# w_ffn_in in 1024-column blocks, with three of eight pairs of K blocks in seven products, and half of their weight sums by accumulating DMA

## The chip, the cores and the metric

The kernel runs on one core of a Trainium2 chip. Its engines are TensorE (matmul; PE in the profile), VectorE (DVE), ScalarE (ACT), GpSimd (POOL) and SyncE (SP); DMAs are issued from the queues of SP, ACT and POOL. The metric is the time of one execution in device microseconds.

## The reference

One layer over 256 tokens of width 2048, all in float32: three gated token mixers with an output projection and a layer norm, then a SwiGLU feed forward of width 5632 and a layer norm. The change lies in the feed forward:

```python
x = layer_norm(DEEPNORM_ALPHA * x + mix, ln_mix_g[l], ln_mix_b[l])
h_gate, h_up = jnp.split(jnp.einsum('bsd,df->bsf', x, w_ffn_in[l]), 2, axis=-1)
ffn = jnp.einsum('bsf,fd->bsd', jax.nn.silu(h_gate) * h_up, w_ffn_out[l])
x = layer_norm(DEEPNORM_ALPHA * x + ffn, ln_ffn_g[l], ln_ffn_b[l])
```

## The kernel before

Every weight passes once through a stream. `load_one` (L98) loads a tile `wraw` of two K blocks of 128 rows by 512 columns, 512 KB, on SP's queue into one of four buffers. `split_one` (L87) splits it exactly into two float32r tiles: ScalarE casts the high part `whi` (L92), VectorE subtracts it from the weight for the low part `wlo` (L94); each has seven buffers. A product of activations and weights is then three matmuls (L118 to L120): high by high, high by low, low by high, with the stationary operand from the transposed activations (`th`, `tl`), and 512 weight columns streamed.

`gemm` (L139) takes one chunk of 512 columns over all of K, for both tiles of 128 tokens: at each weight tile it calls `pump`, which puts loads (five tiles ahead) and splits (three ahead) into the program, and then emits 12 matmuls, 2 K blocks x 2 token tiles x 3. At the chunk's end it evacuates the two PSUM banks. `defer` puts other work behind a number of weight tiles. A Tile scheduler orders the instructions of each engine; an engine then takes its own in that order, and waits at each for what it needs.

The feed forward has three parts (FF_PARTS) of four, four and three rounds. In a round, a gate chunk (`fg`, 16 K blocks) gives silu(gate) (L631, L632), an up chunk (`fu`) multiplies it (L640), and four transposes for each token tile put the result, split, into `hT` (L162 to L169). After the rounds of a part, four chunks of `w_ffn_out` (`fo`) add to the residual R (L652). In the first four rounds `mix_residual` (L617, L618) scales R. Six PSUM banks serve the chunks, two the transposes.

Of the kernel before, what the change touches and what calls it, by code (L numbers as in the profile page):

```python
# [8 lines left out]
F32 = mybir.dt.float32  # L9
F32R = mybir.dt.float32r  # L10
# [28 lines left out]
FF_PARTS = ((0, 4), (4, 8), (8, 11))  # L39

# [7 lines left out]
def trunk_kernel(ctx: ExitStack, tc: tile.TileContext, x, ln_in_g, ln_in_b, w_in, gate_bias,  # L48
# [10 lines left out]
    ps_acc = ctx.enter_context(tc.tile_pool(name="ps_acc", bufs=6, space=PSUM))  # L59
    ps_tp = ctx.enter_context(tc.tile_pool(name="ps_tp", bufs=2, space=PSUM))  # L60
# [22 lines left out]

    raw_t, split_t = {}, {}
    state = {"dma": 0, "split": 0}
    background = []

    def split_one():
        j = state["split"]
        t = raw_t.pop(j)  # L90
        hi = wp.tile([P, KT, NW], F32R, name="whi")
        nc.scalar.copy(out=hi, in_=t)  # L92
        lo = wp.tile([P, KT, NW], F32R, name="wlo")
        (nc.gpsimd if j in POOL_SPLIT else nc.vector).tensor_tensor(out=lo, in0=t, in1=hi.bitcast(F32), op=ALU.subtract)  # L94
        split_t[j] = (hi, lo)
        state["split"] += 1
# [7 lines left out]

    def pump(i):
# [5 lines left out]
        while state["split"] < min(len(plan), i + 1 + SPLIT_AHEAD):  # L111
            split_one()
        for _ in range(min(BACKGROUND, len(background))):
            background.pop(0)()
# [20 lines left out]
    def gemm(key, xs, evac, skew=0):  # L135
        """One 512-column chunk for both token tiles; the second one trails by `skew` weight tiles."""
        first_tile, nk = chunk[key]
        xh, xl = xs
        ps = [ps_acc.tile([P, NW], F32, name="acc") for _ in range(NT)]  # L139
        n = nk // KT  # L140
        for i in range(n + skew):
            if i < n:
                pump(first_tile + i)
            for t, ii in ((0, i), (1, i - skew)):
                if not 0 <= ii < n:
                    continue
                hi, lo = split_t[first_tile + ii]
                for kk in range(KT):
                    k = ii * KT + kk
                    mm_tile(ps[t], xh, xl, t, k, hi, lo, kk, k == 0, k == nk - 1)  # L150
                if ii == n - 1:
                    evac(t, ps[t])
            clock[0] += 1
            run_deferred()
        for i in range(n):
            split_t.pop(first_tile + i)

    def transpose4(src):
        """src [128, 4, 128] -> its four blocks transposed, in one bank."""
        tp = ps_tp.tile([P, 4, P], F32, name="tp")  # L160
# [52 lines left out]
    for f0, f1 in FF_PARTS:  # L213
        for f in range(f0, f1):
            add_chunk(("fg", f), w_ffn_in[0], f * NW, 0, 16)
            add_chunk(("fu", f), w_ffn_in[0], DFF + f * NW, 0, 16)
        for j in range(4):
            add_chunk(("fo", f0, j), w_ffn_out[0], j * NW, f0 * 4, (f1 - f0) * 4)

# [31 lines left out]
    cw = const.tile([P, 8, KC + KA], F32, name="cw")  # L251
    wT = const.tile([P, 8, P], F32, name="wT")
# [4 lines left out]
    # The tensor engine's clock rises only while it works.  # L257
# [11 lines left out]
    def norm_transposed(dst, q, t, src, mu, rs, pg, pb, out_xhat, act=2):  # L269
        """(src - mu) * rs, transposed, then * g + b per channel, split into dst."""  # L270
# [3 lines left out]
        y = blocks(new_tmp())  # L274
# [291 lines left out]
    ffp = None  # L566
    R, x2T = [], []

    def open_ffn():
        nonlocal ffp  # L570
        br.close()
        ffp = ctx.enter_context(tc.tile_pool(name="ffp", bufs=1))
        x2T.extend(new_xt(ffp))
        R.extend(ffp.tile([P, D], F32, name=f"R{t}") for t in range(NT))

    defer(open_ffn)

# [7 lines left out]
    for j in range(4):  # L585
        res = {}

        def residual(j=j, res=res):
            gj, bj = bcast(lg2, j, "gj"), bcast(lb2, j, "bj")
# [9 lines left out]
        def evac_o(t, ps, j=j, res=res):  # L599
# [4 lines left out]
            if j == 3:  # L604
                mu, rs = mean_rstd(stm[t])
                for q in range(4):
                    r_ = R[t][:, cols(q)]
                    norm_transposed(x2T, q, t, r_, mu, rs, PR_MG, PR_MB, r_)
# [3 lines left out]

    def mix_residual(j):
        gj, bj = bcast(ln_mix_g, j, "gj"), bcast(ln_mix_b, j, "bj")
# [6 lines left out]
    stf = stats_tile("stf", 4)  # L621
    f_ln = []
    for f0, f1 in FF_PARTS:
        hT = new_xt(act)
        last_part = f1 * NW == DFF
        for f in range(f0, f1):
            a_ = {}

            def evac_fg(t, ps, a_=a_):
                s_ = a_[t] = new_tmp()  # L630
                nc.scalar.activation(out=s_, in_=ps, func=AF.Sigmoid)  # L631
                nc.vector.tensor_tensor(out=s_, in0=ps, in1=s_, op=ALU.mult)  # L632

            gemm(("fg", f), x2T, evac_fg, skew=SKEW if f == 0 else 0)
            if f < 4:
                defer(lambda f=f: mix_residual(f))

            def evac_fu(t, ps, a_=a_, f=f):
                a = a_[t]
                nc.vector.tensor_tensor(out=a, in0=ps, in1=a, op=ALU.mult)  # L640
                defer(lambda: split_to(hT, 4 * (f - f0), t, transpose4(blocks(a))))

            gemm(("fu", f), x2T, evac_fu)
        if last_part:
            for src in (ln_ffn_g, ln_ffn_b):
                t_ = ffp.tile([P, D], F32, name="fln", bufs=2)
                nc.scalar.dma_start(out=t_, in_=src[0:1].broadcast_to([P, D]))
                f_ln.append(t_)
        for j in range(4):
            def evac_fo(t, ps, j=j):  # L650
                r_ = R[t][:, cols(j)]
                nc.vector.tensor_tensor(out=r_, in0=r_, in1=ps, op=ALU.add)  # L652
                if not last_part:
                    return
                nc.vector.bn_stats(out=stf[t][:, j, :], in_=r_)
                if j < 3:
                    return
                mu, rs = mean_rstd(stf[t])
                for q in range(4):
                    r_ = R[t][:, cols(q)]  # L660
                    nc.vector.scalar_tensor_tensor(out=r_, in0=r_, scalar=mu, in1=f_ln[0][:, cols(q)],
                                                   op0=ALU.subtract, op1=ALU.mult)
                    nc.vector.scalar_tensor_tensor(out=r_, in0=r_, scalar=rs, in1=f_ln[1][:, cols(q)],  # L663
                                                   op0=ALU.mult, op1=ALU.add)
                    (nc.sync, nc.scalar)[q % 2].dma_start(out=out2d[cols(t, P), cols(q)], in_=r_)

            gemm(("fo", f0, j), hT, evac_fo, skew=SKEW_OUT if last_part and j == 3 else 0)
# [30 lines left out]
```

## Time and profile before

| | |
|---|---|
| Time, median of three runs (range) | 1583.06 us (1582.04 to 1583.98) |
| Profiled execution: span from first to last instruction | 1580.9 us |
| TensorE busy | 1558.3 us, 99% |
| VectorE, ScalarE, GpSimd busy | 988.3 us (63%), 669.7 us (42%), 16.7 us |
| DMA | 308.1 MB, 195 GB/s |

The profiled execution is known by its span; the timed runs hold some two microseconds more. Matmuls are pipelined, so the mean time of one in the profile overlaps with the next; its pace is read from the distance of two events. A row of idle time names what an engine waited for last. The engine that is busy nearly all the time sets the end; waits of the others cost nothing as long as it does not wait for them.

### The profile page before, as it was taken

Reading aid. Unit: us, or ns where it says so; the run is one execution under the profiler, and the core shown is the slowest. Engines: PE = TensorE matmul, PEld = TensorE weight load, DVE = VectorE, ACT = ScalarE, POOL = GpSimd, SP = SyncE. Lnnn points to the kernel's source line nnn. Section 1 sums busy time; section 2 is a strip of 40 time slices with the busy share of each in tenths; the row PEclk is TensorE's granted clock in tenths of the full one; section 3 lists DMA queues with packets and bytes.
Section 4 is the critical chain, followed back from the end, with each engine's and each line's share of the span. In section 5 each row is a group of like instructions: output and inputs, shape, how many; then the busy total and the mean of one; then the engine's idle time right before and its main releaser. Section 6 shows DMA issues by size and latency. Waiting matters only on the chain.

```text
span 1580.9 us, 18324 instructions
## 1 busy us (share of the span) xinstructions
PE 1558.3 (99%) x6970; PEld 1280.5 (81%) x6970; DVE 988.3 (63%) x1216; ACT 669.7 (42%) x733; POOL 16.7 (1%) x28
## 2 busy tenths in 40 slices
PE   7999999999999999999999999999999999999997
PEld 4888888888888888888887888888888888888885
DVE  7699999455465555656769655555455554554465
ACT  5444444434444434544336444433444434344431
POOL 1000000000000000000000000000000000000000
PEclk9999999999999999999999999999999999999998
DMA  6866666666666666676866666666666666666652
GB/s 200 284 190 188 185 187 197 200 192 180 199 186 194 205 200 195 198 235 184 286 194 205 202 192 187 187 193 193 190 187 188 185 193 190 198 187 188 186 186 79
DMA packets 159278, 308.10 MB, mean 195 GB/s; under 512 B 9812, under 2 KB 10932, under 8 KB 158934
## 3 DMA queue, kind: packets, MB, share of 16 engines
q1 hardware_dynamic: 153942, 295.38, 62.2%
q10 hardware_dynamic: 5248, 11.55, 2.3%
q8 instruction: 54, 0.88, 0.2%
q14 instruction: 34, 0.28, 0.0%
HBM read 304.80 MB, written 2.10 MB: 194 GB/s over the span
## 4 chain that ended last, share of the span: by engine, by line
PE 97%; DVE 1%; DMA 0%; issue 0%; ACT 0%; POOL 0%; SPq 0%; POOLq 0%; DVEq 0%
PE acc L120 32%; PE acc L118 32%; PE acc L119 31%; PE tp L162 2%; DMA x<-in_x_dram 0%; PE tp L452 0%; DVE tmp L280 0%; DVE tmp L271 0%; DVE tl L169 0%; ACT tmp L278 0%; DVE wlo L94 0%; POOL ve L177 0%; DVE R L663 0%; DVE R L271 0%; PE tp L409 0%
## 5 line engine op out<-in xcount | busy, mean ns | idle before, releaser
L94 DVE TENSOR_TENSOR wlo<-wraw,whi 128x1024 fp32r<-128x1024 f32 x551 | 673.0, 1223 | 556.1 <-ACT whi L92 555.4
L92 ACT CAST whi<-wraw 128x1024 fp32r<-128x1024 f32 x552 | 580.7, 1053 | 835.8 <-PE acc L120 746.9
L118 PE MATMUL acc<-whi,th 128*128 128x512 f32 x2016 | 790.3, 392 | 0.0
L120 PE MATMUL acc<-whi,tl 128*128 128x512 f32 x2016 | 787.9, 391 | 0.0
L119 PE MATMUL acc<-wlo,th 128*128 128x512 f32 x2016 | 786.2, 390 | 0.0
L120 PEld LDWEIGHTS acc<-whi,tl 128*128 128x128 f32 x2016 | 378.8, 188 | 80.8 <-DVE tl L169 0.2
L119 PEld LDWEIGHTS acc<-wlo,th 128*128 128x128 f32 x2016 | 379.0, 188 | 79.7 <-DVE wlo L94 0.3
L118 PEld LDWEIGHTS acc<-whi,th 128*128 128x128 f32 x2016 | 378.9, 188 | 78.5 <-ACT th L168 0.4
L378 DVE SCALAR_TENSOR_TENSOR cv<-pad,cw,cv 128x256 f32<-128x256 f32 x240 | 100.4, 478 | 0.0
L120 PE MATMUL acc<-whi,yl 128*128 128x512 f32 x192 | 76.0, 396 | 0.0
L118 PE MATMUL acc<-whi,yh 128*128 128x512 f32 x192 | 75.8, 395 | 0.0
L119 PE MATMUL acc<-wlo,yh 128*128 128x512 f32 x192 | 75.7, 395 | 0.0
L119 PEld LDWEIGHTS acc<-wlo,yh 128*128 128x128 f32 x192 | 36.2, 188 | 8.5
L120 PEld LDWEIGHTS acc<-whi,yl 128*128 128x128 f32 x192 | 36.2, 188 | 8.4
L118 PEld LDWEIGHTS acc<-whi,yh 128*128 128x128 f32 x192 | 36.2, 188 | 8.2
L162 PE MATMUL tp<-ident,tmp 128*128 128x128 f32 x184 | 25.9, 280 | 8.5 <-DVE tmp L271 7.0
L162 PEld LDWEIGHTS tp<-ident,tmp 128*128 128x128 f32 x184 | 21.9, 143 | 13.0 <-issue 4.6
L177 POOL TENSOR_SCALAR ve<-mv 128x1 f32<-128x1 f32 x8 | 5.0, 623 | 1537.9 <-DVE mv L175 1537.9
L652 DVE TENSOR_TENSOR R<-R,acc 128x512 f32<-128x512 f32 x24 | 15.4, 681 | 6.6 <-PE acc L120 6.6
L169 DVE TENSOR_TENSOR tl<-tp,th 128x512 fp32r<-128x512 f32 x30 | 19.2, 682 | 0.0
L278 ACT ACTIVATE tmp<-tp,prm 128x128 f32<-128x128 f32 x36 | 14.5, 458 | 11.0 <-PE tp L162 10.8
L168 ACT CAST th<-tp 128x512 fp32r<-128x512 f32 x30 | 16.1, 587 | 4.9 <-PE tp L162 4.9
(98 smaller groups left out, 336.2 us busy)
## 6 DMA issues: line engine op xcount, KB each, us to landing
wraw<-in_w_in_dram SPq DMA_DIRECT2D x208, 512.0 KB, 4.2
wraw<-in_w_ffn_in_dram SPq DMA_DIRECT2D x176, 512.0 KB, 3.7
wraw<-in_w_ffn_out_dram SPq DMA_DIRECT2D x88, 512.0 KB, 4.6
wraw<-in_w_branch_dram SPq DMA_DIRECT2D x48, 512.0 KB, 4.6
wraw<-in_w_out_dram SPq DMA_DIRECT2D x32, 512.0 KB, 6.0
gb<-in_gate_bias_dram ACTq DMA_DIRECT2D x12, 256.0 KB, 4.8
tmp<-in_x_dram SPq DMA_DIRECT2D x8, 256.0 KB, 5.9
x<-in_x_dram SPq DMA_DIRECT2D x2, 512.0 KB
```

What stands on the lines that cost most here:

```text
L92: nc.scalar.copy(out=hi, in_=t)
L94: (nc.gpsimd if j in POOL_SPLIT else nc.vector).tensor_tensor(out=lo, in0=t, in1=hi.bitcast(F32), op=ALU.subtract)
L118: nc.tensor.matmul(ps, lhsT=xh[:, k, ts], rhs=hi[:, kk, :], start=first, stop=False)
L119: nc.tensor.matmul(ps, lhsT=xh[:, k, ts], rhs=lo[:, kk, :], start=False, stop=False)
L120: nc.tensor.matmul(ps, lhsT=xl[:, k, ts], rhs=hi[:, kk, :], start=False, stop=last)
L162: nc.tensor.transpose(out=tp[:, b, :], in_=src[:, b, :], identity=ident)
L168: nc.scalar.copy(out=h, in_=src)
L169: nc.vector.tensor_tensor(out=dst[1][:, b0:b0 + 4, cols(t, P)], in0=src, in1=h.bitcast(F32), op=ALU.subtract)
L177: nc.gpsimd.tensor_scalar(out=r, in0=mv[:, 1:2], scalar1=EPS, scalar2=None, op0=ALU.add)
L278: nc.scalar.activation(out=y[:, b, :], in_=tp[:, b, :], func=AF.Identity, scale=g, bias=bb)
L378: nc.vector.scalar_tensor_tensor(out=cv[:, b, :], in0=pad[:, b, q:q + S], scalar=w_, in1=cv[:, b, :], op0=ALU.mult, op1=ALU.add)
L652: nc.vector.tensor_tensor(out=r_, in0=r_, in1=ps, op=ALU.add)
```

## The change

A block is 1024 columns over all of K, for both token tiles, in four PSUM banks; its weight tiles are one K block by 1024 columns, again 512 KB. The rounds are taken two at a time: gate of both, then up of both. The first two gate chunks and the last round (10) stay chunks. The `w_ffn_out` chunks become blocks of two, but for the last two.

In nine blocks (up of rounds 0 and 1; gate and up of rounds 2 and 3, 4 and 5, 6 and 7, 8 and 9) six of the 16 K blocks are taken as three pairs. A pair is a product of 2 x 2 blocks: two token tiles, two K blocks, two halves of columns, eight products in the plain form. It is computed with seven products (Strassen's scheme in Winograd's form), from four sums of activations, made once (`token_sums`, in `xS`), and four sums of weights, made for each pair in `split_pair`. Two of those weight sums are VectorE additions, two are DMAs of 256 KB from POOL's queue that add to their destination: the first adds within the pair's first raw tile, the second onto a copy of a sum that ScalarE made. Sums are split like weights, so a pair splits 3.5 tiles where two tiles split two. Four products go to four banks of their own over the three pairs; after the last pair `gemm_block` combines them (one ScalarE copy, four VectorE operations), and the evacuation adds the result. A block begins with five single tiles (LEAD); the pairs follow with one, then two, then two single tiles behind them.

The eight PSUM banks become two halves of four, used in turn by successive blocks; the four extra banks and the transposes use the half that is not in turn. Broadcast parameters (`gj`, `bj`, `fln` before) now come from the eight temporaries, and the feed forward's tiles take the place of `cw` and `wT`. Source comments are removed.

```diff
+    def add_block(key, src, n0, kt0, nk, pairs=0):
+        rest = nk - 2 * pairs
+        lead = min(LEAD, rest)
+        steps, k = [("one", 2 * pairs + q) for q in range(lead)], 2 * pairs + lead
+        for i in range(pairs):
+            steps.append(("pair", i))
+            upto = 2 * pairs + lead + (rest - lead) * (i + 1) // pairs
+            steps.extend(("one", q) for q in range(k, upto))
+            k = upto
...
+    def split_pair(t0, t1):
+        b12, b11, b22, b21 = t0[:, 0, :], t0[:, 1, :], t1[:, 0, :], t1[:, 1, :]
+        ts = ffp.tile([P, 3, NW], F32, name="tsum", bufs=1)
...
+        add(ts[:, 0, :], b11, b12)
+        if ADDER:
+            nc.gpsimd.dma_start(out=b12, in_=b22, accum_op=ALU.add)
+        else:
+            add(b12, b12, b22)
+        add(ts[:, 1, :], ts[:, 0, :], b22)
+        second = split_tile(t1)
+        if ADDER:
+            nc.scalar.copy(out=ts[:, 2, :], in_=ts[:, 1, :])
+            nc.gpsimd.dma_start(out=ts[:, 2, :], in_=b21, accum_op=ALU.add)
+        else:
+            add(ts[:, 2, :], ts[:, 1, :], b21)
+        low = split_tile(ts[:, 0:2, :])
+        first = split_tile(t0)
+        last = split_tile(ts[:, 2:3, :], 1)
...
+    def gemm_block(key, xs, evac, combos=None):
...
+            if kind == "one":
+                hi, lo = b
+                for i, ((t, n), ps) in enumerate(outs.items()):
+                    product(ps, a_of(q, t), (hi[:, n, :], lo[:, n, :]), first, last)
+                    if last:
+                        evac(i, t, n, ps, adds.get((t, n)))
+            else:
+                if q == 0:
+                    shared = [halves[1].tile([P, NW], F32, name="acc") for _ in range(4)]
+                p1, p5, p6, p7 = shared
+                st, sp = q == 0, q == pairs - 1
+                product(outs[0, 1], a_of(2 * q + 1, 0), b["b21"], first, last)
+                product(outs[0, 0], c_of(q, 3), b["b22"], first, last)
+                product(p5, c_of(q, 0), b["t1"], st, sp)
+                product(p6, c_of(q, 1), b["t2"], st, sp)
+                product(p1, a_of(2 * q, 0), b["b11"], st, sp)
+                product(p7, c_of(q, 2), b["t3"], st, sp)
+                product(outs[1, 1], a_of(2 * q + 1, 1), b["t4"], first, last)
+                if sp:
+                    c1, v, r, w = (ffp.tile([P, NW], F32, name="part", bufs=4) for _ in range(4))
+                    u = new_tmp()
+                    nc.scalar.copy(out=c1, in_=p1)
+                    nc.vector.tensor_tensor(out=u, in0=p6, in1=c1, op=ALU.add)
+                    nc.vector.tensor_tensor(out=r, in0=p5, in1=u, op=ALU.subtract)
+                    nc.vector.tensor_tensor(out=v, in0=u, in1=p7, op=ALU.subtract)
+                    nc.vector.tensor_tensor(out=w, in0=p7, in1=r, op=ALU.add)
+                    adds = {(0, 1): c1, (1, 1): v, (0, 0): r, (1, 0): w}
...
+            if f == 0:
+                add_chunk(("fg", 0), w_ffn_in[0], 0, 0, 16)
+                add_chunk(("fg", 1), w_ffn_in[0], NW, 0, 16)
+            else:
+                add_block(("fg", f), w_ffn_in[0], f * NW, 0, 16, S_PAIRS)
+            add_block(("fu", f), w_ffn_in[0], DFF + f * NW, 0, 16, S_PAIRS)
```

VectorE's order in a round of the feed forward before: L94 is a low part, L640 the product with the gate, L169 the low part of a transposed result.

```order
L94 TENSOR_TENSOR wlo<-wraw,whi 128x1024 x8
L640 TENSOR_TENSOR tmp<-acc,tmp 128x512 x2
L94 TENSOR_TENSOR wlo<-wraw,whi 128x1024 x2
L169 TENSOR_TENSOR tl<-tp,th 128x4x128 x2
L94 TENSOR_TENSOR wlo<-wraw,whi 128x1024 x6
```

VectorE's order now, at the second pair of the up block of rounds 4 and 5 (L146 sums weights, L136 is a low part; `wraw_9130` and `wraw_9144` are the pair's two raw tiles, `tsum_9164` its sums, `wraw_9094`, `wraw_9162` and `wraw_9211` single tiles):

```order
L146 TENSOR_TENSOR tsum_9164<-wraw_9130 128x512
L136 TENSOR_TENSOR wlo_9148<-wraw_9094,whi_9146 128x1024
L146 TENSOR_TENSOR tsum_9164<-tsum_9164,wraw_9144 128x512
L136 TENSOR_TENSOR wlo_9170<-wraw_9144,whi_9168 128x1024
L136 TENSOR_TENSOR wlo_9176<-tsum_9164,whi_9174 128x1024
L136 TENSOR_TENSOR wlo_9180<-wraw_9130,whi_9178 128x1024
L136 TENSOR_TENSOR wlo_9184<-tsum_9164,whi_9182 128x512
L136 TENSOR_TENSOR wlo_9217<-wraw_9162,whi_9215 128x1024
L136 TENSOR_TENSOR wlo_9235<-wraw_9211,whi_9233 128x1024
```

Where one low part per tile stood, a pair has two sums and four low parts, and the last two of them read what a DMA has added to.

SP's order now at the same pair: its two tiles, the single tiles behind it, and the third pair's two tiles (`wraw_9213`, `wraw_9231`); the semaphores DMASW are those of DMAs that POOL issues, DMAHW those of other DMAs.

```order
L190 DMA wraw_9130<-in_w_ffn_in_dram 128x1024 [waits DMAHW3_49,DVE_49,Activation_49]
L190 DMA wraw_9144<-in_w_ffn_in_dram 128x1024 [waits DMASW1_49,DMASW0_49,DMAHW5_49,DVE_49,Activation_49]
L190 DMA wraw_9162<-in_w_ffn_in_dram 128x1024 [waits DMAHW4_49,DVE_49]
L190 DMA wraw_9211<-in_w_ffn_in_dram 128x1024 [waits DMAHW6_49,DVE_49]
L190 DMA wraw_9213<-in_w_ffn_in_dram 128x1024 [waits DMASW3_49,DMAHW0_49,DMASW2_49,DVE_49]
L190 DMA wraw_9231<-in_w_ffn_in_dram 128x1024 [waits DMAHW7_49,DVE_49]
```

The second tile of the pair is loaded into the buffer that both DMAs of the pair before read, and so is the first tile of the next pair.

VectorE's order now at that block's end (L301 to L304 combine the four banks, L818 adds a combination to a block's bank, L829 multiplies by the gate; `wraw_9296` and the four that follow are the next block's first tiles):

```order
L136 TENSOR_TENSOR wlo_9357<-wraw_9296,whi_9355 128x1024
L136 TENSOR_TENSOR wlo_9361<-wraw_9314,whi_9359 128x1024
L136 TENSOR_TENSOR wlo_9379<-wraw_9351,whi_9377 128x1024
L301 TENSOR_TENSOR tmp_9345<-acc_9188,part_9341 128x512
L136 TENSOR_TENSOR wlo_9413<-wraw_9353,whi_9411 128x1024
L302 TENSOR_TENSOR part_9343<-acc_9187,tmp_9345 128x512
L303 TENSOR_TENSOR part_9342<-tmp_9345,acc_9189 128x512
L304 TENSOR_TENSOR part_9344<-acc_9189,part_9343 128x512
L818 TENSOR_TENSOR tmp_9384<-acc_9054,part_9341 128x512
L818 TENSOR_TENSOR tmp_9390<-acc_9055,part_9342 128x512
L829 TENSOR_TENSOR a_9027<-tmp_9384,a_9027 128x512
```

The combinations stand behind the splits of the next block's first four tiles. The next block's first four products go into the four banks that the combinations read.

## Rows read from the trace of the kernel before

**Rows 1.** The page: busy us by engine; the chain that ended last, by engine.
```profile
PE 1558.3 (99%) x6970; PEld 1280.5 (81%) x6970; DVE 988.3 (63%) x1216; ACT 669.7 (42%) x733; POOL 16.7 (1%) x28
...
PE 97%; DVE 1%; DMA 0%; issue 0%; ACT 0%; POOL 0%; SPq 0%; POOLq 0%; DVEq 0%
```

**Rows 2.** Windows, 900 to 1500 us: length, then busy us by engine.
```profile
core 0: us, PE busy (x) PEld busy (x) DVE busy (x) ACT busy (x) POOL busy (x), PEclk, DMA share, GB/s
900.00:1500.00 600.00, 600.00 (x2668) 494.47 (x2667) 309.16 (x289) 246.87 (x254) 0.00 (x0) 1.00 0.64 190
```

**Rows 3.** The chain of waits, 925 to 976 us: start, us, what.
```profile
928.49 0.87 PE tp L162 x8
...
973.31 0.87 PE tp L162 x8
```

**Rows 4.** Waits, 900 to 1500 us: total us, times, longest.
```profile
ACT whi L92 <- PE acc L120: 341.7, 206, 1.7
DVE wlo L94 <- ACT whi L92: 287.7, 217, 1.5
...
SPq L101 <- DVE wlo L94: 502.0, 216, 3.2
```

**Rows 5.** Timelines of ACT and DVE: start us, us, instruction, idle before it.
```profile
901.06 1.05 ACT L92 CAST whi<-wraw 128x1024 fp32r<-128x1024 f32 x1 [1.70 <-PE acc L120]
...
884.83 1.23 DVE L94 TENSOR_TENSOR wlo<-wraw,whi 128x1024 fp32r<-128x1024 f32 x1 [1.51 <-ACT whi L92]
885.98 1.28 DVE L169 TENSOR_TENSOR tl<-tp,th 128x512 fp32r<-128x512 f32 x2
...
902.15 1.23 DVE L94 TENSOR_TENSOR wlo<-wraw,whi 128x1024 fp32r<-128x1024 f32 x1 [1.52 <-ACT whi L92]
903.29 0.68 DVE L632 TENSOR_TENSOR tmp<-acc,tmp 128x512 f32<-128x512 f32 x1
```

**Rows 6.** Windows, 100 to 140 us, where VectorE has its convolution.
```profile
100.00:140.00 40.00, 40.00 (x183) 33.19 (x181) 40.00 (x74) 17.53 (x19) 0.00 (x0) 1.00 0.66 191
```

**Rows 7.** DMA issues over the span: count, KB each, median us to landing.
```profile
wraw<-in_w_ffn_in_dram SPq DMA_DIRECT2D x176, 512.0 KB, 3.7
wraw<-in_w_ffn_out_dram SPq DMA_DIRECT2D x88, 512.0 KB, 4.6
...
gj<-in_ln_mix_g_dram ACTq DMA_DIRECT2D x4, 256.0 KB, 3.9
...
bj<-in_ln_mix_b_dram ACTq DMA_DIRECT2D x4, 256.0 KB, 6.1
out_dram<-R SPq DMA_DIRECT2D x4, 256.0 KB, 2.4
out_dram<-R ACTq DMA_DIRECT2D x4, 256.0 KB, 2.6
```

More of the change, by code (lines that the diff above doesn't have):

```diff
@@ L58, in trunk_kernel, with two_halves, acc_bank, tp_bank @@
     small = ctx.enter_context(tc.tile_pool(name="small", bufs=4))
-    ps_acc = ctx.enter_context(tc.tile_pool(name="ps_acc", bufs=6, space=PSUM))
-    ps_tp = ctx.enter_context(tc.tile_pool(name="ps_tp", bufs=2, space=PSUM))
+    psum = ctx.enter_context(ExitStack())
+    ps_acc = psum.enter_context(tc.tile_pool(name="ps_acc", bufs=6, space=PSUM))
+    ps_tp = psum.enter_context(tc.tile_pool(name="ps_tp", bufs=2, space=PSUM))
+    halves = []
+    def two_halves():
+        psum.close()
+        halves.extend(psum.enter_context(tc.tile_pool(name=f"ps_half{i}", bufs=4, space=PSUM)) for i in range(2))
+    def acc_bank():
+        return (halves[0] if halves else ps_acc).tile([P, NW], F32, name="acc")
+    def tp_bank():
+        if halves:
+            return blocks(halves[1].tile([P, NW], F32, name="acc"))
+        return ps_tp.tile([P, 4, P], F32, name="tp")
     x2d = x.rearrange("b s d -> (b s) d")
@@ L82, in add_chunk @@
             plan.append(src[r0:r0 + KT * P, n0:n0 + NW].rearrange("(k p) n -> p k n", p=P))
+    block = {}
+    fast = set()
+    def add_block(key, src, n0, kt0, nk, pairs=0):
[7 more added lines that the diff above has]
+            k = upto
+        steps.extend(("one", q) for q in range(k, nk))
+        block[key] = []
+        for kind, q in steps:
+            ks = (q,) if kind == "one" else (2 * q, 2 * q + 1)
+            block[key].append((kind, q, len(plan)))
+            if kind == "pair":
+                fast.add(len(plan))
+            for kk in ks:
+                r0 = (kt0 + kk) * P
+                plan.append(src[r0:r0 + P, n0:n0 + 2 * NW].rearrange("p (n c) -> p n c", c=NW))
     raw_t, split_t = {}, {}
@@ L86, in trunk_kernel, with split_tile, add, part @@
     background = []
+    def split_tile(t, n=KT):
+        hi = wp.tile([P, KT, NW], F32R, name="whi")[:, 0:n, :]
+        nc.scalar.copy(out=hi, in_=t)
+        lo = wp.tile([P, KT, NW], F32R, name="wlo")[:, 0:n, :]
+        nc.vector.tensor_tensor(out=lo, in0=t, in1=hi.bitcast(F32), op=ALU.subtract)
+        return hi, lo
+    def split_pair(t0, t1):
+        b12, b11, b22, b21 = t0[:, 0, :], t0[:, 1, :], t1[:, 0, :], t1[:, 1, :]
+        ts = ffp.tile([P, 3, NW], F32, name="tsum", bufs=1)
+        def add(out, a, b):
+            nc.vector.tensor_tensor(out=out, in0=a, in1=b, op=ALU.add)
+        add(ts[:, 0, :], b11, b12)
[13 more added lines that the diff above has]
+        last = split_tile(ts[:, 2:3, :], 1)
+        def part(pair, i):
+            return pair[0][:, i, :], pair[1][:, i, :]
+        return {"b11": part(first, 1), "t3": part(first, 0), "b22": part(second, 0), "b21": part(second, 1),
+                "t1": part(low, 0), "t2": part(low, 1), "t4": part(last, 0)}
     def split_one():
         j = state["split"]
+        if j in fast:
+            split_t[j] = split_pair(raw_t.pop(j), raw_t.pop(j + 1))
+            state["split"] += 2
+            return
         t = raw_t.pop(j)
[L91 to L95, printed above, removed]
+        if j in POOL_SPLIT:
+            hi = wp.tile([P, KT, NW], F32R, name="whi")
+            nc.scalar.copy(out=hi, in_=t)
+            lo = wp.tile([P, KT, NW], F32R, name="wlo")
+            nc.gpsimd.tensor_tensor(out=lo, in0=t, in1=hi.bitcast(F32), op=ALU.subtract)
+            split_t[j] = (hi, lo)
+        else:
+            split_t[j] = split_tile(t)
         state["split"] += 1
@@ L103, in load_one, with may_split @@
         state["dma"] += 1
+    def may_split():
+        j = state["split"]
+        return j in raw_t and (j not in fast or j + 1 in raw_t)
     def pump(i):
@@ L110, in pump @@
             load_one()
-        while state["split"] < min(len(plan), i + 1 + SPLIT_AHEAD):
+        while state["split"] < min(len(plan), i + 1 + SPLIT_AHEAD) and may_split():
             split_one()
@@ L138, in gemm @@
         xh, xl = xs
-        ps = [ps_acc.tile([P, NW], F32, name="acc") for _ in range(NT)]
+        ps = [acc_bank() for _ in range(NT)]
         n = nk // KT
@@ L156, in gemm, with product, a_of, c_of @@
             split_t.pop(first_tile + i)
+        halves.reverse()
+    def product(ps, a, b, first, last):
+        (ah, al), (bh, bl) = a, b
+        nc.tensor.matmul(ps, lhsT=ah, rhs=bh, start=first, stop=False)
+        nc.tensor.matmul(ps, lhsT=ah, rhs=bl, start=False, stop=False)
+        nc.tensor.matmul(ps, lhsT=al, rhs=bh, start=False, stop=last)
+    def gemm_block(key, xs, evac, combos=None):
+        steps = block[key]
+        xh, xl = xs
+        pairs = sum(kind == "pair" for kind, _, _ in steps)
+        outs = {at: acc_bank() for at in ((0, 1), (1, 1), (0, 0), (1, 0))}
+        adds, shared = {}, None
+        def a_of(k, t):
+            return xh[:, k, cols(t, P)], xl[:, k, cols(t, P)]
+        def c_of(i, c):
+            return combos[0][:, c, i, :], combos[1][:, c, i, :]
+        for s_, (kind, q, tile_) in enumerate(steps):
+            pump(tile_)
+            b = split_t.pop(tile_)
+            first, last = s_ == 0, s_ == len(steps) - 1
+            if kind == "one":
[25 more added lines that the diff above has]
+                    adds = {(0, 1): c1, (1, 1): v, (0, 0): r, (1, 0): w}
+            clock[0] += 1 if kind == "one" else 2
+            run_deferred()
+        halves.reverse()
@@ L158, in transpose4 @@
     def transpose4(src):
-        tp = ps_tp.tile([P, 4, P], F32, name="tp")
+        tp = tp_bank()
         for b in range(4):
@@ L273, in norm_transposed @@
         tp = transpose4(blocks(out_xhat))
-        y = blocks(new_tmp())
+        y = blocks(new_tmp()) if y is None else y
         for b in range(4):
@@ L625, in trunk_kernel @@
         last_part = f1 * NW == DFF
[L626 to L634, printed above, removed]
-            if f < 4:
[L636 to L667, printed above, removed]
```

129 lines of the change are left out of this document (114 added, 15 removed).

## The prediction

> **What bounds the kernel now.** I read the page's busy shares and its chain first: TensorE is busy 99% of the span and 97% of the chain that ended last is its matmuls [rows 1]. Then the stretch from 900 to 1500 us, which lies inside the feed forward: TensorE 600 of 600 us at the full granted clock, VectorE 309, ScalarE 247, a DMA share of 0.64 [rows 2]. So only fewer matmuls, or a faster one, shorten this stretch, unless something else falls behind. Two transposes of equal place in successive gate/up rounds stand 44.82 us apart [rows 3]; without the 0.87 us of eight transposes that is 43.95 us for 192 matmuls, 0.229 us each. (Their listed mean of 0.39 us overlaps with the next one and is no pace.) One weight tile is 12 matmuls, 2.75 us.
>
> Last, what runs beside it. ScalarE's high part waits for TensorE to free a buffer, 341.7 us in that stretch, VectorE's low part waits for the high part, 287.7, and the load queue for the low part [rows 4]: the split stands as far ahead as seven buffers let it. The rows of one such tile show the step: high part 1.05 us, low part 1.23 from start to end; back to back VectorE starts a new one 1.14 us after a 1024-column one, and 0.60 after a 512-column one (1.28 less 0.68) [rows 5].
>
> **The change, part by part.** *Matmuls.* Nine blocks are fast: the up block of round 0, gate and up of rounds 2, 4, 6 and 8. Each has three pairs with 21 matmuls for 24. 9 x 3 x 3 = 81 matmuls x 0.229 = 18.5 us off the path. A fast block has 12 x 10 + 21 x 3 = 183 matmuls, 41.9 us, for 192 and 43.95. On TensorE, from its start: five single tiles to 13.7, pair 1 to 18.5, one tile to 21.3, pair 2 to 26.1, two tiles to 31.6, pair 3 to 36.4, two tiles to 41.9. Transposes stay as many as before.
>
> *VectorE and ScalarE.* A pair costs VectorE three sums or splits of 512 columns and three splits of 1024: 3 x 0.60 + 3 x 1.14 = 5.2 us, where two tiles cost 2.3. With ten single tiles, four combinations and eight evacuations of 0.60 a fast block is 15.6 + 11.4 + 7.2 = 34.2 us of 41.9, and that would fit: between 100 and 140 us VectorE is busy 40 of 40 us and TensorE is held up nowhere [rows 6]. ScalarE has 10 x 1.05 + 3 x (3 x 1.05 + 2 x 0.6) + 3 = 26.6 us. What doesn't fit by itself is the order: VectorE's queue now waits, inside each pair, for two DMAs and for loads that these hold back.
>
> *The accumulating DMAs.* 54 of them, 256 KB each. The trace has no such DMA. Nearest rows, from issue to landing [rows 7]: a 256 KB store out of SBUF, 2.4 and 2.6 us, with little else in flight; a 256 KB row block into SBUF beside the weight stream, 3.9; the one issued right behind it, 6.1. Call it L; I take 3.2, halfway between the quiet store and the 3.9, and keep 2.4 and 6.1 as ends. It can't be below the store, since it reads its target as well. On POOL's queue nothing stands behind them but each other; what waits for them stands in VectorE's, ScalarE's and the load queue's order.
>
> The walk, from T, the moment when a pair's second tile has landed and its first DMA is issued. First DMA, high part, low part of the first tile: T + L + 2.3. Second DMA: ScalarE does the second tile's high part (1.05) and copies the sum (0.6), so it is issued at T + 1.7 and lands at T + L + 1.7. Pair 2's second tile is loaded into the buffer that this DMA reads: a load takes 3.7 [rows 7], so T2 = T1 + L + 5.4. Pair 3's second tile comes behind another load, into the buffer freed by pair 2's first low part: 2.3 + 3.7 + about 1.1 for its neighbour, T3 = T2 + L + 7.1. Behind pair 3, the next block's first three tiles land at L + 5.4, 7.1 and 8.8 after T3 (1.76 apart, the share 0.64 of 2.75 us), so the third is split at L + 11.1; then VectorE's order has one combination, a tile, and three more combinations (T3 + L + 14.6), eight evacuations, a tile and the next pair's first sum: T1' = T3 + L + 21.1. Around the block that is 33.6 + 3L, against TensorE's 41.9. Each fast block loses d = 3L - 8.3 us of its lead.
>
> The lead that a run of fast blocks starts with: pair 2's first tile needs a buffer that pair 1 frees after two products, at 13.7 + 1.4, so its low part ends at 17.4 at the earliest, T3 = 22.2, and the last combination at 36.8 + L. TensorE needs that PSUM bank for the fourth product of the next block, at 41.9 + 2.1 = 44.0. Lead 7.2 - L. The output blocks between the runs have no pairs and restore it. Runs: three blocks, four, two. In the third block of run one eight residual operations (4.8 us at 0.60) stand among the sums of its first pair; those of its first block fall where the lead is still set by buffers, and cost nothing.
>
> At L = 3.2, d = 1.3. Run one: 4.0, 2.7, then 1.4 - 4.8, a stall of 3.4 us. Run two: 4.0, 2.7, 1.4, 0.1. Run three: none. Sum: -18.5 + 3.4 = -15.1. The span of the profiled execution, 1580.9, becomes 1565.8; it stands 2.2 under the median of the timed runs, 1583.06, so the time is 1568.
>
> *The rest.* Token sums: 16 short operations on VectorE in the first gate chunk, at most 16 x 0.60 = 9.6 us, with the seven tiles of lead (19 us) as cover. The new PSUM pools: the first block's fourth bank was that of the last gate chunk, read until about the block's start; 0 to 2 us once, taken as 0. Parameter tiles that now come from the eight temporaries: their loads wait longer, behind the same lead. If that cover is gone, a late one costs up to its 6.1 us, once.
>
> **The rivals.** *Everything is hidden.* With L at the store's 2.5, d is below 0, and only 0.1 us is lost: 1564.6. For it: the DMA moves SBUF to SBUF, in rows of 2 KB. Against: the store ran when the stream had ended. The Trainium skill ("DMA: Bandwidth & Descriptors", section Anatomy of one DMA — SWDGE (gpsimd) path) gives 2.0 us plus the bytes at 436 GB/s, an estimate of 2.6 us here, and by it the time would be this one; no run yet shows such a DMA.
>
> *The sums share the engines with the stream.* Its packets go among those of the weights, which already take 0.64 of the engines [rows 2], and L is that of the 256 KB row beside the stream, 3.9. Then d = 3.4; lead 3.3; run one stalls 0.1 + 8.2, run two 0.1 + 3.4 + 3.4, run three 0.1: 15.3 us, and the time is 1580, no change that can be told. For it: the one row of that size beside the stream. Against: that row is read from memory, and these are not. The same page (section Issuing engines are not separate DMA queues) has all DMAs on the same 16 engines, whoever issues them; with its 2.0 us and 0.6 us of moving at the 0.36 that is left, an estimate of 3.7 us, the time would be 1576.
>
> *The sums land late, and it is slower.* The place is the same: VectorE stands in order at the first tile's low part in every pair, the next load stands behind it, and TensorE stands at the next block's first products and at the later pairs. The point from which it decides is L = 4.05, where the stalls reach 18.5 us. At 4.7, d = 5.8: run one 3.3 + 10.6, run two 3.3 + 5.8 + 5.8, run three 3.3, together 32.1 and a time of 1597; at 6.1 it is 61.5 and 1626. For it: 4.6 us for the output weights' loads and 6.1 for the queued row [rows 7]; an addition reads two streams. Against: half the bytes of a weight load.
>
> *It doesn't do what it says*, the matmul count staying: the program's order has 27 groups of three fewer, so this holds no weight. That the pace of 0.229 us changes with the new sequence of weights and columns: same shapes, same number of weight loads; 2 in 100.
>
> **How the numbers follow.** Forecast, L from 2.9 to 3.7: 0.36, 1566 to 1577. Hidden: 0.17. Shared, 3.7 to 4.3: 0.16, of it 0.05 faster, 0.09 the same and 0.02 slower. Late: 0.29. The pace: 0.02, half the same and half slower. A measurement can tell 0.2%, 3.2 us. Faster 0.58, same 0.10, slower 0.32. Range 1562 to 1602: below it lies 0.03, above it (L over 4.9) 0.15.
>
> **What will show it.** The landing time of the DMAs issued on POOL: up to 3.7 as forecast, over 4.1 slower. The load queue waiting for those DMAs in each pair. TensorE idle at the start of the second to fourth block of a run, waiting for a combination, and hardly in the first. Matmul pace 0.229, 81 fewer. Wrong is the forecast if TensorE also waits at first pairs, or in blocks without pairs, or if VectorE waits for ScalarE and not for the DMAs.

## The result: slower

| | before | after |
|---|---|---|
| Median (range) | 1583.2 us (1582.04 to 1583.98) | 1620.43 us (1613.62 to 1622.53) |
| Ratio, 95% interval | | 1.0227 [1.0212, 1.0241] |
| Span of the profiled execution | 1580.9 us | 1611.6 us |

The forecast was 1568, its range ended at 1602, and what came is the rival that it gave 0.29, sums that land late, at more than its price. The profiled execution took 1613.62, the lowest of its four runs, so its trace shows some 7 us less than the median's loss. The clock granted to TensorE, averaged over the span, was 0.994 of full speed in it and 0.988 to 0.990 in the other three (0.995 before); 0.005 of 1612 us is 8 us, so that difference may be the clock's.

The page after, against [rows 1, 7]: busy time, the chain by engine, two kinds of weight loads and the new DMAs (count, KB each, median us from issue to landing).

```profile
PE 1555.2 (97%) x6889; PEld 1262.8 (78%) x6889; DVE 1114.0 (69%) x1412; ACT 730.9 (45%) x831; POOL 64.0 (4%) x82
...
PE 82%; DMA 7%; DVE 6%; issue 3%; ACT 2%; SPq 0%; POOL 0%; POOLq 0%; ACTq 0%; DVEq 0%
...
wraw<-in_w_ffn_in_dram SPq DMA_DIRECT2D x176, 512.0 KB, 3.9
wraw<-in_w_ffn_out_dram SPq DMA_DIRECT2D x88, 512.0 KB, 4.6
...
wraw<-wraw POOLq DMA_DIRECT2D x27, 256.0 KB, 4.1
tsum<-wraw POOLq DMA_DIRECT2D x27, 256.0 KB, 4.6
```

81 matmuls fewer, as worked out. But TensorE's share of the chain went from 97% to 82%, and DMA, next to nothing before, has 7%. The windows of the stretch that was full before [rows 2], after:

```profile
900.00:1500.00 600.00, 571.86 (x2479) 455.93 (x2479) 419.43 (x461) 293.18 (x329) 43.56 (x50) 1.00 0.70 207
```

The granted clock of this stretch is 1.00, rounded, so in this trace the pace is hardly the cause. Inside the feed forward it fell to 0.50 (1.2 GHz) twice, each time right behind a stop of TensorE of about 3.5 us; the first of these, just ahead of the stretch, has 9 matmuls where the full pace gives 15:

```profile
885.60:889.00 3.40, 3.40 (x9) 2.63 (x9) 0.33 (x1) 0.00 (x0) 0.00 (x0) 0.50 0.58 103
```

TensorE does 2479 matmuls in 600 us where it did 2668: 189 x 0.229 = 43 us of its work are missing, of which only 28 show as idle time. A matmul in front of a gap is listed with its whole 0.39 us, 0.16 more than the pace, there are some forty gaps, and more matmuls start late without one. Read lost work from the count. The waits of that stretch, after, against [rows 4]:

```profile
DVE wlo L136 <- ACT whi L134: 157.2, 144, 4.1
ACT whi L134 <- PE acc L257: 129.2, 81, 4.3
...
PE acc L256 <- DVE wlo L136: 8.3, 13, 0.8
PE acc L314 <- DVE a L829: 7.9, 5, 3.5
...
PE acc L255 <- DVE part L302: 3.5, 4, 1.1
...
SPq L190 <- DVE wlo L136: 334.7, 173, 8.1
SPq L190 <- DMA tsum<-wraw: 176.2, 26, 8.8
```

ScalarE waits 129.2 us for TensorE to free a buffer, where it waited 341.7: much of the lead of the splits is used up. SP's queue, which issues the weight loads, now stands 176 us behind the sums' DMAs. TensorE waits for low parts, in front of the transposes (L314) for the gated product, and at the blocks' starts for the combinations (L302, with the rows of L300, L301 and L304 7.9 us).

The new sums can be followed on POOL's queue. Its timeline over the second to fourth block of the second run of fast blocks; L150 is a pair's first sum, L157 its second:

```profile
1169.02 0.87 POOL L150 DMA_DIRECT2D wraw<-wraw  x1 [26.68 <-DVE tsum L146]
1171.17 0.87 POOL L157 DMA_DIRECT2D tsum<-wraw  x1 [1.28 <-ACT tsum L156]
1178.83 0.87 POOL L150 DMA_DIRECT2D wraw<-wraw  x1 [6.79 <-DMA wraw<-in_w_ffn_in_dram]
...
1190.08 0.87 POOL L150 DMA_DIRECT2D wraw<-wraw  x1 [8.93 <-DMA wraw<-in_w_ffn_in_dram]
...
1216.32 0.87 POOL L150 DMA_DIRECT2D wraw<-wraw  x1 [23.96 <-DVE tsum L146]
...
1226.86 0.87 POOL L150 DMA_DIRECT2D wraw<-wraw  x1 [6.91 <-DVE tsum L146]
...
1238.25 0.87 POOL L150 DMA_DIRECT2D wraw<-wraw  x1 [9.09 <-DMA wraw<-in_w_ffn_in_dram]
...
1264.39 0.87 POOL L150 DMA_DIRECT2D wraw<-wraw  x1 [23.87 <-DVE tsum L146]
```

From first pair to first pair: 47.3 and 48.1 us. The walk had 33.6 + 3L, 43.2 at L = 3.2; TensorE needs 41.9, and after every second block 1.7 more for 16 transposes, 42.8 on average.

### The profile page after: what moved, and what is told of

Same layout as the page of the kernel before. It is cut to its first block, busy times and chain, and to the rows that moved or that the text cites. A ratio compares the mean times of both kernels' runs of the same rounds, so it can differ in the third digit from the quotient of the medians.

```text
span 1611.6 us, 18778 instructions
## 1 busy us (share of the span) xinstructions
PE 1555.2 (97%) x6889; PEld 1262.8 (78%) x6889; DVE 1114.0 (69%) x1412; ACT 730.9 (45%) x831; POOL 64.0 (4%) x82
## 4 chain that ended last, share of the span: by engine, by line
PE 82%; DMA 7%; DVE 6%; issue 3%; ACT 2%; SPq 0%; POOL 0%; POOLq 0%; ACTq 0%; DVEq 0%
PE acc L211 18%; PE acc L213 18%; PE acc L212 18%; PE acc L256 9%; PE acc L255 9%; PE acc L257 9%; DVE wlo L136 3%; DMA wraw<-in_w_ffn_in_dram 2%; DMA tsum<-wraw 2%; ACT whi L134 2%; PE tp L314 1%; DMA tmp<-in_x_dram 1%; DMA wraw<-in_w_ffn_out_dram 1%; DVE tmp L818 1%; PE acc L314 1%
## 5 line engine op out<-in xcount | busy, mean ns | idle before, releaser
L136 DVE TENSOR_TENSOR wlo<-wraw,whi 128x1024 fp32r<-128x1024 f32 x551 | 670.5, 1222 | 408.7 <-ACT whi L134 406.7
L211 PE MATMUL acc<-whi,th 128*128 128x512 f32 x1136 | 446.3, 393 | 0.0
L213 PE MATMUL acc<-whi,tl 128*128 128x512 f32 x1136 | 444.5, 391 | 0.0
L212 PE MATMUL acc<-wlo,th 128*128 128x512 f32 x1136 | 443.5, 391 | 0.0
L255 PE MATMUL acc<-whi,th 128*128 128x512 f32 x745 | 296.6, 398 | 15.1 <-DVE a L825 3.6
L256 PE MATMUL acc<-wlo,th 128*128 128x512 f32 x745 | 293.7, 394 | 7.5 <-DVE wlo L136 7.5
L257 PE MATMUL acc<-whi,tl 128*128 128x512 f32 x745 | 291.5, 391 | 0.0
L212 PEld LDWEIGHTS acc<-wlo,th 128*128 128x128 f32 x1136 | 214.2, 189 | 44.7 <-DVE wlo L136 0.6
L213 PEld LDWEIGHTS acc<-whi,tl 128*128 128x128 f32 x1136 | 213.9, 188 | 44.9 <-DVE tl L321 0.2
L211 PEld LDWEIGHTS acc<-whi,th 128*128 128x128 f32 x1136 | 214.1, 189 | 43.6 <-ACT th L320 0.4
L255 PEld LDWEIGHTS acc<-whi,th 128*128 128x128 f32 x745 | 140.2, 188 | 54.6 <-ACT whi L134 7.1
L256 PEld LDWEIGHTS acc<-wlo,th 128*128 128x128 f32 x745 | 140.4, 188 | 41.5 <-DVE wlo L136 13.8
L257 PEld LDWEIGHTS acc<-whi,tl 128*128 128x128 f32 x745 | 140.3, 188 | 30.0
L136 DVE TENSOR_TENSOR wlo<-tsum,whi 128x1024 fp32r<-128x1024 f32 (+1 forms) x54 | 51.6, 956 | 26.4 <-ACT whi L134 26.3
L134 ACT CAST whi<-tsum 128x1024 fp32r<-128x1024 f32 (+1 forms) x54 | 45.0, 833 | 28.0 <-PE acc L257 15.2
L150 POOL DMA_DIRECT2D wraw<-wraw x27 | 23.7, 878 | 554.6 <-DMA wraw<-in_w_ffn_in_dram 234.9
L256 PE MATMUL acc<-wlo,xS 128*128 128x512 f32 x108 | 42.7, 396 | 0.8 <-DVE wlo L136 0.8
```

What stands on the lines that cost most here:

```text
L136: nc.vector.tensor_tensor(out=lo, in0=t, in1=hi.bitcast(F32), op=ALU.subtract)
L150: nc.gpsimd.dma_start(out=b12, in_=b22, accum_op=ALU.add)
L211: nc.tensor.matmul(ps, lhsT=xh[:, k, ts], rhs=hi[:, kk, :], start=first, stop=False)
L212: nc.tensor.matmul(ps, lhsT=xh[:, k, ts], rhs=lo[:, kk, :], start=False, stop=False)
L213: nc.tensor.matmul(ps, lhsT=xl[:, k, ts], rhs=hi[:, kk, :], start=False, stop=last)
L255: nc.tensor.matmul(ps, lhsT=ah, rhs=bh, start=first, stop=False)
```

## The experiments

Theories A (landing times, through the order of VectorE, buffers and loads), B and C are named in the expectations, which stood before each run. All times are medians; before was 1582.6 to 1583.1 in these comparisons.

**Taking the change apart.** Sums by VectorE (`ADDER = False`):

> All four weight sums of a pair on VectorE, no accumulating DMA; the seven products stay. Theory A (the DMAs' landing, 4.1 and 4.6 us in the median where 3.2 was forecast, holds VectorE's order and the loads behind it): the walk around a block has no L left; VectorE's pair costs 6.4 us, links of 7.6, 10.8 and 23.6 us make 42 against TensorE's 41.9, so hardly any stall in the pairs: 1566 to 1575 us. Theory B (VectorE has too much to do in a fast block, and the DMAs relieve it): 3 x 1.2 us more per block, slower than 1620, about 1650 us.

Measured: 1577.69, ratio 0.9962 [0.9947, 0.9977]. The DMAs cost 42.7 us. VectorE has room for the sums. It is still 3 to 12 us above what was expected: something else costs too.

Blocks without pairs (`S_PAIRS = 0`, without `xS`):

> Blocks of 1024 columns, banks in halves and order of evacuation as changed, but no pair takes seven products (no token sums, no weight sums, no DMAs). Theory A: 1583 plus the opening wait of 3.6 us that the changed kernel shows where the first block starts, about 1585 to 1588. Theory C (the blocks themselves cost: four banks evacuated at once, transposes behind them): 1595 to 1610 us.

Measured: 1595.82, 1.0080 [1.0059, 1.0101], 13 us slower than before. TensorE's waits in this run, 690 to 715 us and then 870 to 895 us, where before has nothing of the kind:

```profile
PE tp L314 <- DVE merged L659: 5.3, 1, 5.3
...
PE acc L255 <- DVE a L824: 5.8, 1, 5.8
```

Two single stops, 11 of the 13 us. Right behind each the granted clock is 0.50, from 710.8 to 717.6 and from 888.3 to 895.1 us, which costs some more. So the blocks themselves do not cost their evacuations. The pairs with vector sums gain 1595.82 - 1577.69 = 18.1 us; but the two stops are 2.6 us shorter in the run with vector sums (4.8 and 3.7), so this agrees with the 18.5 of the forecast's first term only within some 3 us.

Only the first sum by DMA (the second by `add(ts[:, 2, :], ts[:, 1, :], b21)`), then only the second (the first by `add(b12, b12, b22)`):

> Of a pair's two accumulating DMAs only the first (within the first raw tile) stays; the second sum is VectorE's. Theory A: the next pair's second tile waits for one DMA issued 1.7 us earlier, so the walk is some 2 to 3 us shorter per block: 1598 to 1610 us, and better than the next run. Theory B: slower than 1620.

> Only the second accumulating DMA stays (onto ScalarE's copy); the first sum is VectorE's. Theory A: the first tile's low part no longer waits for a DMA, but the next loads still wait for the later of the two: 1600 to 1615 us, slower than the run with the first DMA only or equal. Theory B: slower than 1620.

Measured: 1611.14, 1.0185 [1.0167, 1.0203], and 1596.73, 1.0087 [1.0070, 1.0104]: 33 and 19 us over the run without DMAs, together more than both cost at once. The order of the two was expected wrongly, both times lie outside their ranges, and why the first costs more is not settled. In the code it holds both weight buffers of the pair (it reads one and writes the other), the second only one; but SP's queue stands 121.0 us behind the first alone and 162.1 behind the second alone. ScalarE, which takes its high parts in order, stands 52.7 us behind the first alone and 35.6 behind the second alone; this goes the way of the times, but was not tested.

**The two single stops.** The first: `residual` (L762) re-reads x and needs gain and bias rows. Before, these rows lay in the feed forward's own pool, which opens only when the branches' pool closes; now they lie in the temporaries, free much earlier, and the scheduler moves the whole work up. The instruction's row of before, and then of after (first and last start):

```profile
L593 DVE SCALAR_TENSOR_TENSOR tmp<-tmp,mvin,gj x8: 744/748/753, 749.6 to 769.5; 128x512 f32<-128x512 f32 x8
```

```profile
L762 DVE SCALAR_TENSOR_TENSOR tmp<-tmp,mvin x8: 744/752/754, 671.7 to 773.0; 128x512 f32<-128x512 f32 x8
```

On SP's queue after, the re-reads of x stand between weight loads, and VectorE waits for them in its order:

```profile
688.53 0.34 SPq L761 DMA_DIRECT2D tmp<-in_x_dram  x1
689.66 0.37 SPq L190 DMA_DIRECT2D wraw<-in_w_branch_dram  x1
690.33 0.34 SPq L761 DMA_DIRECT2D tmp<-in_x_dram  x1
691.46 0.37 SPq L190 DMA_DIRECT2D wraw<-in_w_branch_dram  x1
```

```profile
684.57 0.75 DVE L762 SCALAR_TENSOR_TENSOR tmp<-tmp,mvin 128x512 f32<-128x512 f32 x1 [2.82 <-DMA tmp<-in_x_dram]
...
704.69 2.52 DVE L136 TENSOR_TENSOR wlo<-wraw,whi 128x1024 fp32r<-128x1024 f32 x2 [1.22 <-ACT whi L134]
707.13 1.28 DVE L658 TENSOR_TENSOR gate<-acc,gate 128x512 f32<-128x512 f32 x2
708.33 1.28 DVE L659 TENSOR_TENSOR merged<-merged,gate 128x512 f32<-128x512 f32 x2
```

The transposes at 709 wait for that last line; 1.8 us in this trace, 5.3 in the one without pairs. The repair, on the run with vector sums:

```diff
-    def bcast(src, j):
-        t_ = new_tmp()
+    def bcast(src, j, part=False):
+        t_ = ffp.tile([P, NW], F32, name="part", bufs=4) if part else new_tmp()
...
-            gj, bj = bcast(lg2, j), bcast(lb2, j)
+            gj, bj = bcast(lg2, j, True), bcast(lb2, j, True)
```

> All sums on VectorE, as in the run e1 (1577.7 us), and the gain and bias rows of the input norm in buffers that exist only once the branch buffers are closed, as before the change, and not in the eight temporaries. Theory W: in the temporaries these loads and the re-reads of x can be issued while branch C still runs; SyncE's queue then waits with them ahead of weight loads, and TensorE stops 5 us at 707. With the old buffers that stop goes: 1572 to 1575, no gap over 1.5 us between 660 and 860. Rival: VectorE's own load makes the gap, and it stays or moves: 1576 to 1579.

Measured: 1571.23, 0.9926 [0.9913, 0.9940], 6.5 us off, where the stop itself was 4.8 us in the run with vector sums; behind it the granted clock was 0.50 from 709.6 to 716.4 us. L762 is back at its old place and the stop is gone:

```profile
L762 DVE SCALAR_TENSOR_TENSOR tmp<-tmp,mvin,part x8: 743/746/752, 748.9 to 772.2; 128x512 f32<-128x512 f32 x8
```

The second stop is the new PSUM pools: they open when the old ones close, so the first block waits for the last evacuation of the gate chunk ahead of it. TensorE's wait at 870 to 895 us in the changed kernel:

```profile
PE acc L255 <- DVE a L825: 3.6, 1, 3.6
```

The repair keeps four banks in a pool of their own from the start:

```diff
-    ps_acc = psum.enter_context(tc.tile_pool(name="ps_acc", bufs=6, space=PSUM))
+    ps_a = ctx.enter_context(tc.tile_pool(name="ps_a", bufs=4, space=PSUM))
+    ps_b = psum.enter_context(tc.tile_pool(name="ps_b", bufs=2, space=PSUM))
...
-        halves.extend(psum.enter_context(tc.tile_pool(name=f"ps_half{i}", bufs=4, space=PSUM)) for i in range(2))
+        halves.extend([ps_a, psum.enter_context(tc.tile_pool(name="ps_half1", bufs=4, space=PSUM))])
```

> As the last one, and the first block's four PSUM banks are a pool that is open from the start, so that it needs no banks of the gate chunk just ahead of it. Theory: the 4.1 us stop ahead of the first block was the wait for all banks at once, 1568 to 1571, that is 12 to 15 us faster than before the change. Rival: loads are late there and the stop moves behind the first products of the block: 1572 to 1575.

Measured: 1565.54, 0.9891 [0.9877, 0.9904], another 5.7 us. In the run before it the stop was 3.9 us, and behind it, from 884.7 to 888.1 us, the granted clock was 0.50: eight matmuls there start every 0.43 us in place of 0.229, another 1.6 us. Here a stop cost more than its own length. The page of this run (busy, chain) and then its windows show the kernel that the first term of the forecast described, near the 1564.6 of its rival "everything is hidden":

```profile
PE 1540.8 (99%) x6889; PEld 1265.4 (81%) x6889; DVE 1140.9 (73%) x1466; ACT 714.3 (46%) x804; POOL 16.7 (1%) x28
...
PE 87%; DVE 8%; DMA 2%; ACT 1%; issue 1%; SPq 0%; POOL 0%; POOLq 0%; DVEq 0%; ACTq 0%
```

```profile
900.00:1500.00 600.00, 599.07 (x2665) 492.30 (x2664) 466.60 (x531) 294.48 (x322) 0.00 (x0) 1.00 0.62 201
```

Both repairs under the DMA sums:

> The changed kernel with both repairs, sums by accumulating DMA as in the change. Theory: the two stops (2.2 and 3.6 us in it) go and the 43 us that the sums by DMA cost (1620.4 against 1577.7) stay: 1611 to 1616, 40 to 46 over the run without them. Rival: part of the 43 us is made by the same two stops, 33 to 39 over it.

Measured: 1611.70, 1.0181 [1.0167, 1.0195]. So the sums by DMA cost 46.2 us with the stops repaired. The repairs give 8.7 us here, not the 12.2 they gave without the DMAs, so the two costs are apart only within some 3.5 us. Some of the 46.2 us is the clock: in this trace it is 0.50 from 1299.3 to 1306.1 and from 1487.0 to 1493.8 us, behind stops where runs of fast blocks end, an estimate of 6 us (33 matmuls, 0.2 us more each); without the DMAs it stays full from 20 to 1556 us.

**Landing time or buffers.** Each DMA moving half of its sum, VectorE the other half:

```diff
+            add(b12[:, 0:H], b12[:, 0:H], b22[:, 0:H])
-            nc.gpsimd.dma_start(out=b12, in_=b22, accum_op=ALU.add)
+            nc.gpsimd.dma_start(out=b12[:, H:], in_=b22[:, H:], accum_op=ALU.add)
```

and the same for the second sum, whose copy by ScalarE is halved too.

> Four weight buffers and both repairs (1611.7 us by DMA), where each DMA takes 256 of the 512 columns of its sum, 128 KB, and VectorE the other 256. Theory S (a landing that is x us shorter gives up to 27 x us, 3 in each of 9 blocks): with the landing at 3.0 to 3.6 in place of 4.0 and 4.4, 1585 to 1600. Rival F (the landing is a fixed cost, bytes hardly count): landing within 0.3 us of before, 1604 to 1615.

Measured: 1600.16, 1.0101 [1.0080, 1.0123], 11.5 us less. The first and second sum's landing, min, median and max, first with 256 KB, then with 128 KB:

```profile
DMA to landing us min/median/max: 3.3/4.0/7.6
...
DMA to landing us min/median/max: 3.3/4.4/6.7
```

```profile
DMA to landing us min/median/max: 2.7/3.5/6.1
...
DMA to landing us min/median/max: 2.6/3.1/5.2
```

The median fell by 0.5 and 1.3 us; 27 x 0.5 = 13.5 for the first sum alone, near the 11.5. The time stands at the upper end of what theory S said. The other way, the first sum's DMA issued twice, so that b22 is added twice:

> Four weight buffers and both repairs (1611.7 us), with the first sum's accumulating DMA issued twice, one behind the other, so that one of the weight sums has b22 added twice and the output is another. Theory S (three landings in a row in each block): with about 4 us more for each of 27, 60 to 108 us slower, 1670 to 1720. Rival (loads and buffers, not the landing, set the pace; the two DMAs run side by side): 1612 to 1640.

Measured: 1676.18, 1.0599 [1.0568, 1.0630], 64.5 us more. POOL's wait for the DMA before it, and the landing of the doubled one:

```profile
POOL wraw L155 <- DMA wraw<-wraw: 54.7, 21, 4.8
```

```profile
DMA to landing us min/median/max: 3.2/3.3/5.8
```

The two run one behind the other: 27 x 3.3 = 89 us more of landing. But the 64.5 us are not the landing's alone. TensorE now stops often, and its clock falls; the windows of this run:

```profile
900.00:1500.00 600.00, 538.93 (x2209) 428.24 (x2208) 364.42 (x401) 257.75 (x291) 57.49 (x66) 0.93 0.69 194
```

The granted clock is 0.50 in 92 us of the profiled execution, against 14 with the sum issued once. Some 190 matmuls start in these 92 us; at 0.2 us more for each, an estimate, that is up to 38 us, and 6 us with the sum issued once. The profiled execution is 72 us longer. So the time goes with the landing, as theory S says; how much of it comes straight from the landing, and how much from the clock behind the stops, this run does not part: between (72 - 32) / 89 = 0.45 and 64.5 / 89 = 0.7 of each microsecond.

Six weight buffers in place of four in the feed forward, under the DMA sums (two more in `ffp`, `wraw2`; loads two tiles further ahead; three of the four `part` tiles in temporaries):

> The changed kernel with both repairs and six buffers for incoming weights in the feed-forward part in place of four (loads two tiles further ahead); three of the four part results go to the temporaries to make room. Theory R (a fast pair holds its two buffers until its sum has landed, and the loads of the next tiles queue behind it): 20 to 40 us faster than the run with four buffers, 1572 to 1595. Theory Q (VectorE takes its work in order and stands behind the landing; the one buffer for sums does the rest): within 6 us of it, 1606 to 1618.

> The run with six weight buffers (1578.6 us), with all sums on VectorE: what the two more buffers do without the DMAs (1565.5 us with four). Theory R (the buffers only give back what the held ones cost): 1563 to 1567, so that 12 to 15 us remain as the price of the DMAs. Rival: two more buffers are worth several us by themselves, 1556 to 1562, and the price of the DMAs with six buffers is then larger.

Measured: 1578.63, 0.9972 [0.9961, 0.9982] with DMA sums, and 1563.08, 0.9874 [0.9860, 0.9889] with vector sums. Two buffers take the price of the DMAs from 46.2 to 15.5 us, while the landings are no shorter (first sum, then second):

```profile
DMA to landing us min/median/max: 3.3/4.3/8.1
...
DMA to landing us min/median/max: 3.3/5.7/8.0
```

That parts the two theories: most of the price is what a held weight buffer does to the loads behind it, with the low clock that followed (with six buffers the clock is full from 20 to 1568 us), and VectorE's order and the single `tsum` buffer are at most the last 15.5. Nor do the sums' bytes explain it: both kernels move the same, and in the median a load of `w_ffn_in` lands, from 900 to 1500 us, in 4.2 us without the DMAs, 4.4 with them and four buffers, 4.3 with six.

**One pair more**, with vector sums and both repairs (`S_PAIRS = 4`, one `part` tile in a temporary; by `add_block` the first two pairs of a block then stand next to each other, and only the others have a tile between them):

> The fastest so far (1565.5 us: sums on VectorE, both repairs) with four of eight pairs fast in place of three: 27 matmuls fewer at 0.229 us, 6.2 us. Theory (TensorE sets the time, VectorE has room): 1559 to 1562. Rival (four pairs with one other tile between them need more weight tiles than the buffers hold): 1566 to 1580.

Measured: 1575.87, 0.9957 [0.9942, 0.9972], 10.3 us slower than with three. From 900 to 1500 us TensorE waits for high and low parts, which it hardly does with three pairs:

```profile
PE acc L259 <- ACT whi L138: 8.1, 14, 1.9
PE acc L260 <- DVE wlo L140: 3.7, 5, 2.1
```

Whether split or weight buffers run out there was not taken apart. The best version is three pairs, vector sums, both repairs and six buffers: 1563.08 us, 20 us under before.

## Why the prediction was wrong

- *Matmuls, 18.5 us*: right. 81 fewer; with vector sums and both stops repaired the kernel is 17.1 us under before.
- *VectorE's 34.2 us in a block fit*: right, as the runs with all sums on VectorE show; with both repairs it is busy 466.60 of 600 us and TensorE 599.07.
- *The step that failed: "L; I take 3.2"*. The DMA lands in 3.3 us at the least, 4.1 and 4.6 in the median, on the other side of the deciding point, 4.05, that the prediction itself gave. The quiet end of the bounds, the store [rows 7], came from a stretch without the weight stream; all 54 sums run beside it (DMA share 0.70). The row beside the stream, 3.9, was the nearer one. By the rule of the Trainium skill ("DMA: Bandwidth & Descriptors", Anatomy of one DMA — SWDGE (gpsimd) path), 2.6 us, the cost would have been hidden; the trace disagrees even with its shortest landing, 3.3. The shared engines of the Trainium skill (the same page, Issuing engines are not separate DMA queues), with the estimate of 3.7, came closer.
- *The walk's constants* are short as well. By it, 4.1 to 4.6 gives 1584 to 1595 (between its 18.5 us of stalls at 4.05 and 32.1 at 4.7), and with the two stops, 5.4 us, 1589 to 1600, still 20 to 31 us below; some 7 us of this may be the clock of the three slower executions. Links measured against the walk: from first to second pair 9.8 and 10.5, second to third 11.3 and 11.4, third to the next block's first 26.2 and 26.1. The first sums' three landings in these two blocks add up to 12.2 and 11.0 us, for which the walk gives 45.8 and 44.6 around the block; 47.3 and 48.1 came. So of the 4.5 us by which a block's 47.7 stand above the forecast's 43.2, 2.0 are L and some 2.5 the constants; these were not traced to single steps. In the other direction, d leaves out TensorE's transposes: it needs 42.8 on average, not 41.9.
- *Lead 7.2 - L*: the lead itself was not measured, but L is not one number. In the first block of that run the third pair's sums landed in 6.4 and 6.0 us (DMA share 0.91 from the issue to the landing of the first), and by the rule the lead is then 0.8, not 4.0. Inside the runs ScalarE's copies that open the combinations show the loss; the second run's four, after and then in the repaired kernel with vector sums:

```profile
L300 ACT COPY part<-acc x4: 578/580/586, 1155.8 to 1302.1; 128x512 f32<-128x512 f32 x4
```

```profile
L304 ACT COPY part<-acc x4: 575/579/582, 1133.0 to 1263.2; 128x512 f32<-128x512 f32 x4
```

  48.8 against 43.4 us a block. Run one has 97.0 against 87.0 for its two intervals, run three 48.0 against 42.8: together 31 of the 48.3 us between the two spans. The two stops make 5.4; the rest stands in the runs' first blocks and behind their last ones.
- *A wait that it left out*: the transposes behind an up block need its gated product, and TensorE waited for it five times, 7.9 us in the stretch, 3.5 at the longest.
- *A cost that no term has*: TensorE's clock. Behind the two longest stops it was 0.50, for 6.8 us together in this trace; by their mean clock it was lower for longer in the three slower executions.
- *The signs*: the load queue stood behind the DMAs, as the forecast said, and TensorE at the blocks' starts and at later pairs. One sign of being wrong came too: VectorE's waits are put down to ScalarE (157.2 us), none to the DMAs. It is ScalarE, first in the order with the high parts, that stands at the landings (12.7 and 4.3 us). But VectorE waited for ScalarE before the change as well [rows 4], so this sign could tell nothing.
- *The rest*: the new PSUM pools were taken as 0, with 2 as the most; the stop was 3.6 us, and its repair gave 5.7. The parameter tiles were thought of as loads that could be late, hidden by the lead. They were early instead, and brought the re-reads of x in front of weight loads; 1.8 us here. The repair gave 6.5 in the run with vector sums, where the stop was 4.8. The sum of the terms taken as nothing was 12 us in the repaired line of kernels.
- *Rivals*: "lands late" is what happened, by its place (loads behind the DMA, TensorE at the blocks' starts and later pairs); only its price was too small, and the two stops had no place in it.

## What to carry to other kernels

A DMA that sits between a load and the reuse of its buffer is paid in buffers: count how long each buffer is held, and either add buffers or leave the work on an engine with room. A tile moved to another pool changes when the scheduler can start what fills it; look at where its instructions went, its DMAs' queue included, before calling the move free. Bound an unseen DMA by rows from the stretch in which it will run.

## What was not expected of the hardware

An accumulating DMA between buffers of SBUF, issued on POOL's queue, takes POOL 0.87 us and lands in 2.6 to 2.7 us at the least with 128 KB and in 3.3 with 256 KB (3.2 in two runs). A line through 2.65 and 3.3, an estimate from the shortest landings of two sizes, gives 0.65 us for 128 KB, 202 GB/s, and 2.0 us without bytes. The Trainium skill ("DMA: Bandwidth & Descriptors", Anatomy of one DMA — SWDGE (gpsimd) path) has the same 2.0 us, but 436 GB/s; by this estimate the bytes go at half of that. Among the weight loads the same DMA took up to 7.6 us with four weight buffers and 8.1 with six.
